# One projection unit for latent queries, keys and forget gates, and a router's weight sums by two wide products

## The chip, the cores and the metric

The kernel runs on one core of one Trainium2 chip. The metric is the device time of one execution in microseconds. Engines are TensorE (PE; its weight loads are PEld), VectorE (DVE), ScalarE (ACT), GpSimd (POOL) and SyncE (SP), which issues most DMAs.

## What is computed

A decoder trunk of two layers over 512 tokens of width 1024, in float32. Of each layer the parts that matter here are the input projection, from which the latents and forget gates come, and the router:

```python
def _mixing(x, w_in, b_forget, g_cq, g_ckv, w_uq, w_ukv, g_head, w_out):
    proj = x @ w_in                                   # 1024 x 4260
    p_sb, p_fox, p_mla, p_dil = jnp.split(proj, ...)
    q, k, v, f = jnp.split(p_fox, [hd, 2 * hd, 3 * hd], axis=-1)
    log_f = jax.nn.log_sigmoid((f + b_forget))        # 4 columns: forget gates
    c_q, c_kv, k_r = jnp.split(p_mla, [256, 384], axis=-1)   # 256, 128 and 32 columns
    q = (_rmsnorm(c_q, g_cq) @ w_uq)
    kv = (_rmsnorm(c_kv, g_ckv) @ w_ukv)
...
def _hier_moe(x, w_group, b_group, w_expert, b_expert, w1, w3, w2):
    g_logits = xf @ w_group + b_group                 # 4 groups
    e_logits = xf @ w_expert + b_expert               # 16 experts, top-1 group, top-2 inside
```

Four kinds of attention (stick-breaking, forgetting, latent, dilated) share the projection; then a norm, the routed experts, and a second norm.

## The kernel before

Tokens lie in four tiles of 128 (`NT`). The residual stream is held transposed, as xT, in two halves (a rounded part and the rest), and every weight piece is loaded by SP, split by `hi` (ScalarE) and `lo` (VectorE, a subtraction of two SBUF tiles) in `Stream.conv_to` (lines 547 to 567), and multiplied in three passes (`mm3`, line 394). A projection unit (`Unit`, line 727) is a block of columns of `w_in`; `unit_parts` (line 591) cuts it into pieces of 4 x 128 rows where it has up to 256 columns, else of 2 x 128. A unit of kind "tok" makes 24 products per token tile (8 row blocks, three passes), with xT as the weight of TensorE and the columns streamed.

`ORDER` (line 597) gives the units' order. Its first two are "cq" (256 columns: latent queries) and "ckv" (160: latent keys and the rotary key, with the 4 forget-gate columns copied behind them by ScalarE, 164 in all). `projections` (line 867) goes through `lists_` (lines 862 and 863): the first `N_MIX` units tile by tile (cq 0, ckv 0, cq 1, ...), then the other units one after the other. `un.begin()` asks for the conversion of all the unit's pieces and of one piece ahead; a unit's first tile therefore stands behind all of these in ScalarE's and VectorE's queues, though a product waits only for its own piece. `ev_latent` (line 804) copies a tile's bank to SBUF and sums its squares on ScalarE. Then `mla_rest` (line 1072) transposes the forget gates and goes on to the rotary keys, and `mla_prep` (line 1122) normalises both latents; both wait for the events of all four tiles. `fox_consts` waits for the unit that `FC_AT` names.

All order is made by a planner in the kernel (`Plan`, line 88) while the program is built. Each chain of work is a generator that yields what it needs (pages of SBUF, banks of PSUM, events); the planner keeps a clock for each engine by costs of its own and always runs the chain that could start first. Its choice fixes the order of every engine's queue. The projections are "fill": of chains that could start by now on TensorE, another one goes first. `convert_first` (line 1555) converts the first pieces of a layer as early as they come, four in layer 0, two in layer 1 (`FIRST_CONV`).

At the start of layer 1 the second norm of layer 0 (`second_norm`, line 1591) delivers xT tile by tile: eight transposes on TensorE, scale and shift and the two halves on ScalarE and VectorE (`second_norm_T`), while GpSimd makes the stored copy by a product and a sum over 1024 columns (`second_norm_out`), which may begin when the tile's transposes are done.

`router_weights` (line 1438) scales the router's 20 columns by the norm's gain and shift (`wg`, `wb`, 8 row blocks of 20 columns each) and sums them over all 1024 rows: a matrix of ones times each block, 16 products of 20 columns accumulated into one bank. The sums, `wsum`, are first read by the first norm (line 1513). A float32 product is two instructions on PE.

Nearly every row names line 250, where a helper records every instruction, so rows are told apart by tiles and shapes.

Of the kernel before, what the change touches and what calls it, by code (L numbers as in the profile page):

```python
# [14 lines left out]
OP = mybir.AluOpType  # L15
# [15 lines left out]
N_PAGES = 42  # L31
FC_AT = "ckv"
N_PG = 12
N_MIX = 2
MAX_ITEMS = 4
# [41 lines left out]
def trunk(ctx, tc, x, w_in, b_forget, g_cq, g_ckv, w_uq, w_ukv, g_head, w_out, ln1_g, ln1_b,  # L77
# [513 lines left out]
    def unit_parts(w, c0, n, extra=None):  # L591

        kn = 2 if n > 256 else 4
        return [ws.add(cols(w, c0, n, kn * i, kn), kn, n,
                       None if extra is None else extra[:, kn * i:kn * i + kn, :]) for i in range(8 // kn)]

    ORDER = ["cq", "ckv", "d1q", "d1k", "d1v", "sbq", "sbk", "sbv", "d23q", "d23k", "d23v", "fxq", "fxk", "fxv"]
    COL = {"sbq": (0, 256), "sbk": (256, 256), "sbv": (512, 256), "fxq": (768, 256), "fxk": (1024, 256),
           "fxv": (1280, 256), "cq": (C_CQ, 256), "ckv": (C_CKV, 160)}
    for j, s in enumerate("qkv"):  # L600
        COL[f"d1{s}"] = C_DIL + 768 * j, 256
        COL[f"d23{s}"] = C_DIL + 768 * j + 256, 512
    for l in range(L):
        for u in ORDER:
            win_u[l, u] = unit_parts(w_in[l], *COL[u], wfs[l] if u == "ckv" else None)
        wo = w_out[l].rearrange("(g k p) c -> g p k c", g=4, k=2)
# [100 lines left out]
    def attention(l, x_ready, xT, x_stored):  # L707
# [96 lines left out]
        def ev_latent(un, b, i):  # L804
            n, c = (256, 0) if un.u == "cq" else (128, 1)
            nc.scalar.activation(un.out[0][:, i, 0:b.shape[1]], b, AF.Copy)
            nc.scalar.activation(b[:, 0:n], b[:, 0:n], AF.Square, scale=float(n) ** -0.5,
                                 accum_out=lat_ss[:, 2 * i + c:2 * i + c + 1])

        kinds = {"cq": ("tok", 1, ev_latent), "ckv": ("tok", 1, ev_latent)}  # L810
        for u, n in (("d1", 1), ("d23", 2)):
# [55 lines left out]
        def projections():  # L867
            for u, i in lists_:
                un = U[u]
                evs = [x_ready[i]] if un.kind == "tok" and not un.perm else list(x_ready)  # L870
                yield Need(pages=un.pages, banks=1, evs=evs)
                un.begin()
                if un.kind == "tok":
                    b = bank([128, 164 if u == "ckv" else COL[u][1]])
                    un.mm(b, i, range(8))
                else:
                    b = bank([128, 512])
                    un.mm(b, i, range(4))
                    yield Need()
                    un.mm(b, i, range(4, 8))  # L880
                un.end(b, i)
# [190 lines left out]
        def mla_rest():  # L1072
            yield Need(pgs=2, banks=1, evs=[ev["ckv"]])
            ckt = U["ckv"].out[0]

# [46 lines left out]
        def mla_prep():  # L1122
# [3 lines left out]
            nc.gpsimd.dma_start(wqr, w_uq[l].rearrange("(k p) c -> p k c", p=128))  # L1126
            cqt, ckt = U["cq"], U["ckv"]
            yield Need(evs=[ev["cq"], ev["ckv"]])
            cqt, ckt = cqt.out[0], ckt.out[0]
            v, y = st(8), st(8)  # L1130
# [307 lines left out]
        def router_weights():  # L1438
# [6 lines left out]
            yield Need(banks=1)  # L1445
            b = bank([128, 2, 20])
            for n, w in enumerate((wg, wb)):
                for k in range(8):
                    nc.tensor.matmul(b[:, n], lhsT=full, rhs=w[:, k], start=n == 0 and k == 0, stop=n == 1 and k == 7)
            yield Need()  # L1450
            nc.vector.tensor_copy(wsum, b)
            nc.vector.tensor_tensor(wsum[:, 1], wsum[:, 1], br, op=OP.add)
# [239 lines left out]
    for l in range(L + 1):  # L1692
# [473 lines left out]
        def last_rows(last):  # L2166
# [13 lines left out]
            if l + 1 == L:  # L2180
                load_gb(last, nc.sync)
            else:
                ws.limit = win_u[l + 1, ORDER[2]][-1] + 1

# [233 lines left out]
```

## Time and profile before

| | |
|---|---|
| median of 3 runs | 1615.7 us (1611.23 to 1615.98) |
| the profiled execution's own time | 1619.65 us |
| its span, first to last instruction | 1617.7 us |
| PE busy | 1436.7 us, 89%, 7620 products |
| PE weight loads busy | 1164.3 us, 72% |
| DVE, ACT, POOL busy | 68%, 55%, 23% |
| mean granted clock of TensorE | 0.929 |

Attention of layer 0 runs up to about 330 us, its output projection, norm and routing to about 450, the experts to about 765; layer 1 follows in the same way. A granted clock of 1.00 is 2.4 GHz and 0.50 is 1.2 GHz. Busy shares are means over stages with different limits, so the rows below are read by stage. In a row of the timeline, merged instructions have one row; its start and the start of the next row are used for rates.

### The profile page before, as it was taken

How to read it: one execution, taken by the hardware profiler on the slowest of the kernel's cores; microseconds unless marked ns; L12 is line 12 of the kernel's file. 1: busy time of each engine (PE TensorE's matmuls, PEld its weight loads, DVE VectorE, ACT ScalarE, POOL GpSimd, SP SyncE). 2: the span in 40 equal slices, each digit the busy share in tenths (PEclk: the TensorE clock that was granted, in tenths of full speed). 3: DMA queues.
4: the chain of work that ended last, by engine and by line, in shares of the span. 5: the costliest groups of instructions: out<-in, count | busy, mean ns of one | idle time of the engine just before them, and what ended most of it. 6: DMA issues, size and time to landing. Idle time of an engine off the chain costs nothing. (4 is left out here: it accounts for less than half of the span.)

```text
span 1617.7 us, 22596 instructions
## 1 busy us (share of the span) xinstructions
PE 1436.7 (89%) x7620; PEld 1164.3 (72%) x7620; DVE 1099.8 (68%) x1967; ACT 890.5 (55%) x1695; POOL 368.7 (23%) x388
## 2 busy tenths in 40 slices
PE   7999989989799999888799998989786999899674
PEld 7988878878666767655699987878666667666453
DVE  4745575476686889977774546654658779898667
ACT  5435454434346888775543534545424477887553
POOL 2511120240412224311421112002204213323002
PEclk9989999999899999988798999989887999999797
DMA  9201211263579999985330102204545799999813
GB/s 266 65 1 41 89 42 40 83 232 143 195 264 319 370 379 356 377 318 173 105 90 23 40 27 92 65 21 134 213 166 195 263 355 382 386 347 385 302 34 130
DMA packets 120700, 303.54 MB, mean 188 GB/s; under 512 B 21982, under 2 KB 45230, under 8 KB 120568
## 3 DMA queue, kind: packets, MB, share of 16 engines
q1 hardware_dynamic: 106936, 269.74, 45.9%
q0 software_dynamic: 12448, 32.11, 7.1%
q8 instruction: 64, 1.05, 0.3%
q14 instruction: 68, 0.56, 0.1%
q10 hardware_dynamic: 1184, 0.08, 0.1%
HBM read 284.14 MB, written 27.33 MB: 193 GB/s over the span
## 5 line engine op out<-in xcount | busy, mean ns | idle before, releaser
L250 PE MATMUL bank<-page,page 128*128 128x512 f32 (+5 forms) x4480 | 983.1, 371 | 62.1 <-DVE page L250 35.0
L250 PEld LDWEIGHTS bank<-page,page 128*128 128x128 f32 (+2 forms) x4480 | 760.6, 203 | 197.9 <-DVE page L250 55.2
L250 DVE TENSOR_TENSOR page<-page,page 128x1024 fp32r<-128x1024 f32 (+3 forms) x470 | 525.7, 1163 | 154.3 <-ACT page L250 140.8
L250 ACT ACTIVATE page<-page 128x1024 fp32r<-128x1024 f32 (+3 forms) x454 | 436.2, 1021 | 49.1 <-DMA page<-in_w_in_dram 11.8
L250 PE MATMUL bank<-page,pg 128*128 128x64 f32 (+1 forms) x1360 | 317.0, 375 | 32.3 <-ACT page L250 14.7
L250 PEld LDWEIGHTS bank<-page,pg 128*128 128x128 f32 x1360 | 227.0, 202 | 115.1 <-issue 37.8
L250 ACT ACTIVATE page<-bank 64x512 fp32r<-64x512 f32 (+8 forms) x255 | 122.1, 506 | 197.1 <-PE bank L250 135.7
L250 ACT ACTIVATE pg<-bank 128x256 f32<-128x256 f32 (+6 forms) x223 | 101.4, 469 | 223.5 <-PE bank L250 221.6
L250 POOL DMA_INDIRECT yd<-page,xidx x30 | 67.5, 2249 | 403.3 <-ACT page L250 165.9
L250 DVE TENSOR_TENSOR page<-bank,page 128x512 fp32r<-128x512 f32 (+4 forms) x142 | 79.9, 599 | 65.9 <-ACT page L250 65.7
L250 POOL TENSOR_TENSOR page<-pg,pg 128x256 f32<-128x256 f32 (+1 forms) x56 | 51.1, 928 | 270.0 <-DVE pg L250 211.5
L250 PE MATMUL bank<-cid,pg 128*128 128x128 f32 (+2 forms) x500 | 84.2, 286 | 29.4 <-ACT pg L250 19.4
L250 POOL TENSOR_TENSOR page<-page,page 128x1024 f32<-128x1024 f32 (+4 forms) x32 | 63.1, 1971 | 153.4 <-ACT page L250 104.7
L250 PE MATMUL bank<-cid,page 128*128 128x128 f32 (+1 forms) x608 | 86.5, 280 | 10.5 <-DVE page L250 5.4
L250 PEld LDWEIGHTS bank<-cid,pg 128*128 128x128 f32 (+2 forms) x500 | 58.7, 147 | 46.2 <-ACT pg L250 25.1
L250 PEld LDWEIGHTS bank<-cid,page 128*128 128x128 f32 (+1 forms) x608 | 71.6, 143 | 24.9 <-DVE page L250 7.7
L250 ACT ACTIVATE pg<-pg 128x256 f32<-128x256 f32 (+5 forms) x146 | 68.6, 477 | 22.3 <-DVE pg L250 18.4
L250 POOL DMA_INDIRECT page<-x1d,xidx x30 | 54.5, 1818 | 42.4 <-DVE e_slots L250 17.9
L250 POOL CAST page<-page 64x512 fp32r<-64x512 f32 x48 | 29.9, 623 | 136.3 <-ACT page L250 102.8
L250 DVE COPY pg<-bank 128x256 f32<-128x256 f32 (+3 forms) x73 | 35.2, 484 | 28.4 <-PE bank L250 28.2
L250 DVE TENSOR_TENSOR pg<-bank,pg 64x512 f32<-64x512 f32 (+6 forms) x81 | 44.8, 559 | 11.9 <-ACT pg L250 10.8
L250 POOL MEMSET page<- 128x1024 f32 (+1 forms) x34 | 44.7, 1319 | 1.8 <-DVE page L250 1.8
(217 smaller groups left out, 974.4 us busy)
## 6 DMA issues: line engine op xcount, KB each, us to landing
page<-in_w_dram SPq DMA_DIRECT2D x396, 512.0 KB, 10.9
page<-in_w_in_dram SPq DMA_DIRECT2D x64, 512.0 KB, 4.1
page<-in_w_out_dram SPq DMA_DIRECT2D x16, 512.0 KB, 4.1
x1d<-page SPq DMA_DIRECT2D x8, 512.0 KB, 2.8
yd<-page SPq DMA_DIRECT2D x8, 512.0 KB, 5.1
page<-yd SPq DMA_DIRECT2D x8, 512.0 KB, 7.0
scr<-pg POOLq DMA_DIRECT2D x16, 132.0 KB, 2.0
pg<-scr POOLq DMA_DIRECT2D x16, 132.0 KB, 4.5
```

Of the source, the lines that this page charges most:

```text
L250: r = f(*args, **kw)
```

## The change

The units "cq" and "ckv" become one unit "lat" of 416 columns (they are neighbours in `w_in`) and the 4 forget-gate columns, 420 in all, in four pieces of 2 x 128 rows instead of two and two of 4 x 128. Its two output pages are those of the old units. `N_MIX` is 1, so `lists_` goes lat 0, lat 1, lat 2, lat 3. All that waited for one or both of the old events waits for the new one. The router's sums are made by two products of 160 columns (all eight blocks side by side), and VectorE adds the eight blocks from PSUM, where it copied 40 sums before.

```diff
--- before.py
+++ after.py
@@ -29,9 +29,9 @@
 RMS_EPS = 1e-6
 ALPHA = (2.0 * L) ** 0.25
 N_PAGES = 42
-FC_AT = "ckv"
+FC_AT = "lat"
 N_PG = 12
-N_MIX = 2
+N_MIX = 1
 MAX_ITEMS = 4
 AHEAD = 5
 SPARE = 1
@@ -594,15 +594,15 @@
         return [ws.add(cols(w, c0, n, kn * i, kn), kn, n,
                        None if extra is None else extra[:, kn * i:kn * i + kn, :]) for i in range(8 // kn)]
 
-    ORDER = ["cq", "ckv", "d1q", "d1k", "d1v", "sbq", "sbk", "sbv", "d23q", "d23k", "d23v", "fxq", "fxk", "fxv"]
+    ORDER = ["lat", "d1q", "d1k", "d1v", "sbq", "sbk", "sbv", "d23q", "d23k", "d23v", "fxq", "fxk", "fxv"]
     COL = {"sbq": (0, 256), "sbk": (256, 256), "sbv": (512, 256), "fxq": (768, 256), "fxk": (1024, 256),
-           "fxv": (1280, 256), "cq": (C_CQ, 256), "ckv": (C_CKV, 160)}
+           "fxv": (1280, 256), "lat": (C_CQ, 416)}
     for j, s in enumerate("qkv"):
         COL[f"d1{s}"] = C_DIL + 768 * j, 256
         COL[f"d23{s}"] = C_DIL + 768 * j + 256, 512
     for l in range(L):
         for u in ORDER:
-            win_u[l, u] = unit_parts(w_in[l], *COL[u], wfs[l] if u == "ckv" else None)
+            win_u[l, u] = unit_parts(w_in[l], *COL[u], wfs[l] if u == "lat" else None)
         wo = w_out[l].rearrange("(g k p) c -> g p k c", g=4, k=2)
         wout_u[l] = {(n, g): ws.add(wo[g, :, :, 512 * n:512 * n + 512], 2, 512)
                      for n, g in [(0, 0), (0, 2), (0, 3), (1, 0), (1, 2), (1, 3), (0, 1), (1, 1)]}
@@ -802,12 +802,13 @@
             split_k(un.out, i, b)
 
         def ev_latent(un, b, i):
-            n, c = (256, 0) if un.u == "cq" else (128, 1)
-            nc.scalar.activation(un.out[0][:, i, 0:b.shape[1]], b, AF.Copy)
-            nc.scalar.activation(b[:, 0:n], b[:, 0:n], AF.Square, scale=float(n) ** -0.5,
-                                 accum_out=lat_ss[:, 2 * i + c:2 * i + c + 1])
-
-        kinds = {"cq": ("tok", 1, ev_latent), "ckv": ("tok", 1, ev_latent)}
+            for o, c, w in zip(un.out, (0, 256), (256, 164)):
+                nc.scalar.activation(o[:, i, 0:w], b[:, c:c + w], AF.Copy)
+            for c, n in ((0, 256), (1, 128)):
+                nc.scalar.activation(b[:, 256 * c:256 * c + n], b[:, 256 * c:256 * c + n], AF.Square,
+                                     scale=float(n) ** -0.5, accum_out=lat_ss[:, 2 * i + c:2 * i + c + 1])
+
+        kinds = {"lat": ("tok", 2, ev_latent)}
         for u, n in (("d1", 1), ("d23", 2)):
             kinds[u + "q"] = kinds[u + "k"] = ("tok", n, ev_rope)
             kinds[u + "v"] = ("tok", n, ev_copy)
@@ -871,7 +872,7 @@
                 yield Need(pages=un.pages, banks=1, evs=evs)
                 un.begin()
                 if un.kind == "tok":
-                    b = bank([128, 164 if u == "ckv" else COL[u][1]])
+                    b = bank([128, 420 if u == "lat" else COL[u][1]])
                     un.mm(b, i, range(8))
                 else:
                     b = bank([128, 512])
@@ -1070,8 +1071,8 @@
         mla = {}
 
         def mla_rest():
-            yield Need(pgs=2, banks=1, evs=[ev["ckv"]])
-            ckt = U["ckv"].out[0]
+            yield Need(pgs=2, banks=1, evs=[ev["lat"]])
+            ckt = U["lat"].out[1]
 
             fb = bank([128, 512])
             for t in range(NT):
@@ -1124,9 +1125,8 @@
             wkr, wqr = page([128, 512]), page([128, 2, 384])
             nc.gpsimd.dma_start(wkr, w_ukv[l])
             nc.gpsimd.dma_start(wqr, w_uq[l].rearrange("(k p) c -> p k c", p=128))
-            cqt, ckt = U["cq"], U["ckv"]
-            yield Need(evs=[ev["cq"], ev["ckv"]])
-            cqt, ckt = cqt.out[0], ckt.out[0]
+            yield Need(evs=[ev["lat"]])
+            cqt, ckt = U["lat"].out
             v, y = st(8), st(8)
             rs_v(v, lat_ss, 1.0, RMS_EPS)
             rs_act(y, v)
@@ -1443,12 +1443,11 @@
             for o, s in ((wg, lng[l][0]), (wb, lnb[l][0])):
                 nc.vector.tensor_tensor(o, wr, s.unsqueeze(2).to_broadcast([128, 8, 20]), op=OP.mult)
             yield Need(banks=1)
-            b = bank([128, 2, 20])
+            b = bank([128, 2, 8, 20])
             for n, w in enumerate((wg, wb)):
-                for k in range(8):
-                    nc.tensor.matmul(b[:, n], lhsT=full, rhs=w[:, k], start=n == 0 and k == 0, stop=n == 1 and k == 7)
+                nc.tensor.matmul(b[:, n], lhsT=full, rhs=w, start=n == 0, stop=n == 1)
             yield Need()
-            nc.vector.tensor_copy(wsum, b)
+            nc.vector.tensor_reduce(wsum, b.rearrange("p n k c -> p n c k"), axis=AX.X, op=OP.add)
             nc.vector.tensor_tensor(wsum[:, 1], wsum[:, 1], br, op=OP.add)
             rel(b, full, wb)
 
@@ -2180,7 +2179,7 @@
             if l + 1 == L:
                 load_gb(last, nc.sync)
             else:
-                ws.limit = win_u[l + 1, ORDER[2]][-1] + 1
+                ws.limit = win_u[l + 1, ORDER[N_MIX]][-1] + 1
 
         def load_gb(last, q):
             last.gb = [page([128, D]) for _ in range(2)]
```

## Rows read from the trace of the kernel before

**Rows 1.** TensorE's waits, 0 to 400 us: waiter, released by, sum, times, longest.

```profile
PE bank L250 <- ACT pg L250: 12.9, 12, 5.6
PE bank L250 <- DVE page L250: 7.1, 5, 2.7
...
PE bank L250 <- ACT page L250: 3.2, 2, 2.6
PE bank L250 <- DVE pg L250: 1.0, 1, 1.0
```

**Rows 2.** TensorE's timeline, layer 0: start, length, operation, count, [idle before, released by].

```profile
10.71 4.32 PE L250 MATMUL bank<-page,page 128*128 128x256 f32 x23 [0.68 <-DVE page L250]
...
22.97 16.90 PE L250 MATMUL bank<-page,page 128*128 128x164 f32 x144
39.70 0.60 PE L250 MATMUL bank<-cid,page 128*4 128x128 f32 x4
40.06 3.11 PE L250 MATMUL bank<-page,page 128*128 128x256 f32 x24
43.01 0.60 PE L250 MATMUL bank<-cid,page 128*128 128x128 f32 x4
```

**Rows 3.** Busy time by stretch in the expert stage: PE, PEld, DVE, ACT, POOL, PEclk, DMA, GB/s.

```profile
600.00:700.00 100.00, 93.56 (x406) 66.14 (x405) 88.44 (x108) 80.84 (x106) 36.38 (x18) 1.00 0.99 368
```

**Rows 4.** TensorE's timeline at the start of layer 1.

```profile
767.50 1.88 PE L250 MATMUL bank<-page,cid 128*128 128x512 f32 x4
...
777.07 4.92 PE L250 MATMUL bank<-page,page 128*128 128x256 f32 x22 [3.21 <-DVE page L250]
781.82 1.04 PE L250 MATMUL bank<-cid,page 128*128 128x128 f32 x8
...
813.60 10.94 PE L250 MATMUL bank<-page,page 128*128 128x256 f32 x70 [3.23 <-DVE page L250]
824.38 0.60 PE L250 MATMUL bank<-cid,page 128*4 128x128 f32 x4
```

**Rows 5.** TensorE's timeline, twelve products of 512 columns and the row behind.

```profile
126.66 3.01 PE L250 MATMUL bank<-page,page 128*128 128x512 f32 x12
129.51 0.60 PE L250 MATMUL bank<-cid,page 128*96 128x128 f32 x4
```

**Rows 6.** TensorE's timeline at the router's weight sums, layer 0, then layer 1.

```profile
81.68 1.93 PE L250 MATMUL bank<-wg,pg 128*128 128x20 f32 x16
83.46 2.68 PE L250 MATMUL bank<-pg,pg 128*128 128x20 f32 x19
85.94 4.23 PE L250 MATMUL bank<-page,page 128*128 128x512 f32 x12
90.00 0.52 PE L250 MATMUL bank<-pg,pg 128*128 128x256 f32 x3
...
871.42 1.91 PE L250 MATMUL bank<-wg,pg 128*128 128x20 f32 x16
...
876.00 0.45 PE L250 MATMUL bank<-cid,pg 128*128 128x128 f32 x1
...
880.55 4.64 PE L250 MATMUL bank<-page,page 128*128 128x512 f32 x12
...
885.03 0.60 PE L250 MATMUL bank<-cid,pg 128*128 128x128 f32 x4
```

**Rows 7.** Busy time and granted clock (PEclk) of four short stretches.

```profile
866.00:868.00 2.00, 2.00 (x19) 1.84 (x18) 2.00 (x7) 0.73 (x4) 0.00 (x0) 1.00 0.00 0
87.00:88.00 1.00, 1.00 (x3) 0.78 (x3) 0.00 (x0) 0.00 (x0) 0.00 (x0) 0.50 0.00 0
877.00:878.00 1.00, 1.00 (x7) 0.91 (x6) 0.42 (x1) 0.66 (x2) 0.00 (x0) 0.50 0.00 0
816.00:818.00 2.00, 2.00 (x11) 2.00 (x11) 0.00 (x0) 0.00 (x0) 0.00 (x0) 0.50 0.63 177
```

**Rows 8.** VectorE's timeline, then GpSimd's, start of layer 1.

```profile
779.08 0.84 DVE L250 TENSOR_TENSOR page<-page,page 128x656 fp32r<-128x656 f32 x1
...
783.71 5.67 DVE L250 TENSOR_TENSOR page<-page,page 128x656 fp32r<-128x656 f32 x2 [0.52 <-ACT page L250]
...
783.00 5.30 POOL L250 TENSOR_TENSOR page<-page,page 128x1024 f32<-128x1024 f32 x2 [5.67 <-ACT page L250]
```

**Rows 9.** TensorE's timeline at the routing sums, layer 0, then layer 1.

```profile
444.79 0.19 PE L250 MATMUL bank<-asb,tri 128*128 128x16 bf16 x1 [9.77 <-DVE asb L250]
...
1239.54 0.19 PE L250 MATMUL bank<-asb,tri 128*128 128x16 bf16 x1 [10.03 <-DVE asb L250]
```

## What the change should do to the time

> **What bounds the kernel now.** I read the page's busy shares and its PE waits first, then TensorE's order of time around the two edits, then the clock of the same stretches, then the queues of VectorE and GpSimd at the start of layer 1.
>
> In the first 400 us TensorE waits some 24 us on other engines: 12.9 for ScalarE's softmax tiles, 7.1, 3.2 and 1.0 for others [rows 1]. From 22.97 to 39.70 and beyond, its rows follow one another with no wait shown [rows 2]. So in attention of layer 0 TensorE's own queue sets the pace, and work taken out of it should move what follows. The expert stage that comes after is busy on PE (93.56 of 100 us) and has its DMA full (share 0.99) [rows 3]; both are paced by buffers that earlier work gives back, so a shift made before it should pass through it, and I count it neither as a gain nor as a loss.
>
> The start of layer 1 is another matter. There TensorE waits again and again for VectorE (3.21 us before 777.07, 3.23 before 813.60) [rows 4]: the second norm delivers xT tile by tile, and the latent products of one tile are done before the next arrives. What is saved there is mostly saved on idle time.
>
> **Latent units.** Per token tile, 24 products of 256 columns and 24 of 164 become 24 of 420. In layer 0, 144 products, half of each width, take 16.73 us from 22.97 to 39.70: 232 ns a pair [rows 2]. 24 of 256 columns take 2.95 us from 40.06 to 43.01: 123 ns [rows 2]; so 164 columns cost 110, hardly less, which is why a merge pays at all. No row has 420 columns. Twelve of 512 take 2.85 us from 126.66 to 129.51: 237 ns [rows 5], an upper end; 512 columns scaled down in proportion give 195, the lower end; the line from 123 at 256 to 237 at 512 gives 196, which I take, as it lies on the two nearest widths. Saving 36 ns a pair (-5 to 37), 0.87 us a tile. For tiles 1 to 3 of layer 0 that is 2.6 us (-0.4 to 2.7). Tile 0 is paced by the weights' conversions: 23 products of 256 take 10.71 to about 14.9 after a wait for VectorE [rows 2], 181 ns each. Its four loads stay at the head of SP's queue and carry the same bytes (4 of 426 KB against 2 of 524 and 2 of 328). The wide unit needs all four pieces in its first tile where the narrow one needed two; the pieces keep their bytes (4 of 128x840 against 2 of 1024 and 2 of 656 words a partition), so their last one is converted at the same time. I take 0.4 us gain (-1 to 2). Layer 0: 3.0 us.
>
> ScalarE's and VectorE's conversions handle as many elements as before; two more copies of a few forget-gate columns a layer and the four evacuation operations now in one chain hang on banks that TensorE doesn't need next: nothing on the path, while TensorE has other banks; without that cover, under 1 us a layer. The waits on one event instead of two end where they did, since tile 3 of both units came last anyway.
>
> **Router weight sums.** 16 products of 20 columns (32 instructions on PE) become two of 160 (4). In layer 0 the old ones run from 81.68 to 85.94 with three products of 256 columns among them: 4.26 - 3 x 0.123 = 3.9 us; in layer 1 from 871.42 to 876.00, 4.6 us [rows 6]. TensorE does nothing else meanwhile, so this is path. The new price isn't in the trace: two float32 products of 512 columns take 1.88 us [rows 4], the upper end; two at the price of the narrow ones (3.9/16) 0.5, the lower; in proportion to the columns between these, 0.9. Gain 3.0 and 3.7 us.
>
> Behind the narrow products the clock falls. The granted clock is 1.00 at 866 to 868 and 0.50 at 877 to 878; in layer 0 it is 0.50 at 87 to 88 [rows 7]: half, the lower of its two levels, though PE was busy without a gap, with weight loads and 20 columns apiece. Twelve products of 512 columns then take 85.94 to 90.00, 4.06 us, and 880.55 to 885.03, 4.48 us [rows 6], against 2.85 [rows 5]: 1.2 and 1.6 lost. What runs from 876.00 to 880.55 is slowed too; at the ratio 4.48/2.85 its 4.55 us would be 2.9: 1.7 more. I expect the clock to stay up when the long run of narrow products is gone, since nothing else in these rows is thin: 1.2 + 3.3 us, with zero as the lower end if it falls anyway, and 1.2 + 3.9 as the upper (4.55 halved). Router in all: 4.2 us in layer 0, 7.0 in layer 1.
>
> The copy of 40 sums becomes a strided sum over 320 PSUM elements on VectorE; its result is read only at the first norm, hundreds of us later, so some 0.3 us more of VectorE is covered. Uncovered it would cost just that.
>
> **What passes through.** 3.0 + 4.2 + 7.0 = 14.2 us leave TensorE's queue in attention. Some will come back as waits for softmax tiles, which TensorE now meets earlier [rows 1]; half is my lower end, all the upper, three quarters my value, nearer to all because only 24 us in 400 are waits: 10.7 us (7.1 to 14.2).
>
> **Start of layer 1.** Here PE runs at half clock (0.50 at 816 to 818 [rows 7]): 22 products of 256 columns take 777.07 to 781.82, 216 ns each [rows 4]. At that level width is paid in full (216 scaled to 420 columns: 354, to 164: 138, together 354), so the merge saves nothing until the clock rises. Of the last tile and what follows it, 813.60 to 824.38 [rows 4], I count 0.6 us (0 to 0.9). The hand-over between tiles I put at zero: the transposes of tile 1 come at 781.82, behind the narrow query unit of tile 0, and would come behind the whole wide unit, 24 x (354 - 216) = 3.3 us later at that clock. Against this, the conversions of the second half, which now stand on VectorE between the transposes of tile 1 and the next xT (two subtractions in 5.67 us at 783.71, where one alone took 0.84 [rows 8]), are asked for at the start of the wide unit, ahead of GpSimd's 5.30 us of affine [rows 8], and run in idle time. The two are about equal. Ends: 9.9 us lost (3.3 three times), 6 us gained (5.67 less the 2.2 that two such subtractions take alone, at the first tile, and somewhat less at the other two together).
>
> Those two subtractions, of 656 and 1024 columns, took 5.67 us while GpSimd's two products took 5.30; one of 656 alone took 0.84, and scaled by width the pair would take 2.2 [rows 8]. The Trainium skill, SBUF — State Buffer, "Who interferes with whom", has it that a VectorE operation with two inputs in SBUF and a GpSimd operation that reads SBUF exclude each other for a whole instruction. The trace agrees (5.67 us against 2.2). By that rule two more subtractions of the wide unit would lose up to one affine operation each, 2 x 2.65 us, if they fell there; that is the wide-unit rival below with 5.3 us on top.
>
> **Sum.** 10.7 + 0.6 = 11.3 us off the profiled execution's 1619.65: 1608.4. That execution lies 4 us above the median of 1615.7, which gives 1604.4 as the median after.
>
> **Rivals.**
> - More comes through: the longer first unit lets the transposes of tiles 1 and 2 run together, the hand-over gains its 6 us and all 14.2 pass: 1615.7 - 14.2 - 0.6 - 6 = 1594.9. For it: the subtractions at 783.71 get out of GpSimd's way; against: no row shows the new order.
> - The edit of the router doesn't hold the clock up: 4.5 us less times three quarters, 1607.8. Against: the row at 866 to 868.
> - The gain goes back into softmax waits: a quarter passes, 3.6 + 0.6: 1611.5. For it: 12.9 us of such waits; against: they are few and far apart.
> - The wide unit stands before the transposes at half clock on three tiles: 9.9 us lost, 1614.3. For it: the rows at 777.07 and 781.82; against: the conversions that get out of the way.
> - Slower, by order. The planner sorts all queues by its own clock, which these edits move by several us a layer. What order is worth, the two layers show: from the transposes of the forget gates to the routing sums, the same work takes 405.1 us in layer 0 (39.70 to 444.79) and 415.2 in layer 1 (824.38 to 1239.54) [rows 2, 4, 9]: 10.1 us. The place is the interleaving of softmax items and projections in attention. One layer falling from the better to a worse order eats 10.1: 1614.5. If both do, 20.2 less 11.3: 1624.6. It decides from 16 us on, 11.3 and the 4.8 that can be told from nothing. Against it: a new order can as well be better, above all in layer 1.
>
> **How the numbers follow.** Forecast 0.46; more 0.12; clock falls anyway 0.07; back into waits 0.08; wide unit 0.08; worse order in one layer 0.08; in both 0.11. Under 0.3% (4.8 us) a measurement of this kernel can't be told from no change. The first three are faster: 0.65. The next three are within: 0.24. The last is slower: 0.11. The range goes from 1594 (just past the first rival) to 1618 (the wide unit's 1614.3 with the lower end of what passes, 3.6 us worse); the worse order in both layers and little else are left out.
>
> **What would show it.** Right: 96 latent products a layer near 196 ns in layer 0; four thin router instructions under 1.5 us and a granted clock of 1.00 after them in both layers; the forget gates' transposes 3 us earlier in layer 0; the routing sums some 6 us earlier after them in layer 0. Wrong: more TensorE wait for ScalarE's tiles by as much as was saved; a first tile of layer 1 whose next transposes come later than 5 us after its first product and xT that follows later; a longer way from 824 to the routing sums.

## The result

The changed kernel takes 1627.7 us as the median of six executions (1622.2 to 1632.6); the kernel before, beside it on the same chip, 1614.7 (1611.2 to 1618.7). The ratio is 1.008, with a 95% interval of 1.005 to 1.010: slower by 0.8%, where 1604.4 us had been forecast. The profiled execution of after took 1622.2, below its median, that of before 1619.65, above its own, so the two traces differ by less than the kernels do. In a second set of executions on another chip (below) the ratio was 1.012 [1.008, 1.015]. Three executions that lie far off, one of lat_good (4698.8 us), one of pin_pages (4703.2) and one of the kernel before beside them (1941.4), are left out of all medians.

TensorE has less to do, and finishes later. Its waits in the first 420 us, to be held against [rows 1], which read the same up to 420:

```profile
PE bank L250 <- ACT pg L250: 13.0, 10, 3.9
PE bank L250 <- ACT page L250: 9.2, 4, 3.6
PE bank L250 <- POOL page L250: 7.0, 7, 3.4
...
PE bank L250 <- DVE page L250: 3.8, 6, 1.7
PE bank L250 <- DVE pg L250: 2.9, 7, 0.7
```

ScalarE's softmax tiles (pg) cost what they did; 7.0 us of waits for GpSimd are new, and ScalarE's pages cost 6 us more. TensorE's timeline in layer 0, to be held against [rows 2, 6, 9]:

```profile
20.36 16.89 PE L250 MATMUL bank<-page,page 128*128 128x420 f32 x96
37.09 0.52 PE L250 MATMUL bank<-cid,page 128*4 128x128 f32 x3
38.71 0.27 PE L250 MATMUL bank<-cid,page 128*4 128x128 f32 x1 [1.11 <-ACT page L250]
...
86.18 0.44 PE L250 MATMUL bank<-wg,pg 128*128 128x160 f32 x2
86.45 0.43 PE L250 MATMUL bank<-pg,pg 128*128 128x160 f32 x2
86.62 3.02 PE L250 MATMUL bank<-page,page 128*128 128x512 f32 x12
89.48 0.60 PE L250 MATMUL bank<-cid,page 128*128 128x128 f32 x4
...
461.35 0.20 PE L250 MATMUL bank<-asb,tri 128*128 128x16 bf16 x1 [10.02 <-DVE asb L250]
```

The edits do their own work. The forget gates' transposes begin at 37.09 instead of 39.70, 2.6 us earlier. The four router instructions take 0.44 us (86.18 to 86.62), and the twelve products of 512 columns behind them 2.86 (to 89.48) instead of 4.06, at the upper clock (columns as in [rows 3]):

```profile
87.00:88.00 1.00, 1.00 (x6) 0.83 (x5) 0.92 (x1) 0.63 (x2) 0.00 (x0) 1.00 0.87 328
```

Yet the routing sums of layer 0 come at 461.35, 16.6 us later than in [rows 9]. What has changed is the order. The tile den_m holds the latent attention's softmax, m_str the mask of stick-breaking. These are their rows in layer 0: operation, tile, count, shortest/median/longest ns, first to last start. First those of the kernel before:

```profile
L250 DVE TENSOR_REDUCE den_m<-bank x16: 291/486/692, 133.3 to 168.6; 128x1 f32<-128x128 f32 x4, 128x1 f32<-128x256 f32 x4, 128x1 f32<-128x384 f32 x4, 128x1 f32<-128x512 f32 x4
L250 PE MATMUL bank<-m_str,cidb x16: 229/230/233, 175.8 to 250.3; 128*128 128x128 bf16 x16
```

And those of the changed kernel:

```profile
L250 DVE TENSOR_REDUCE den_m<-bank x16: 280/488/692, 232.2 to 282.8; 128x1 f32<-128x128 f32 x4, 128x1 f32<-128x256 f32 x4, 128x1 f32<-128x384 f32 x4, 128x1 f32<-128x512 f32 x4
L250 PE MATMUL bank<-m_str,cidb x16: 229/230/330, 157.2 to 229.4; 128*128 128x128 bf16 x16
```

Before, the latent attention goes first and stick-breaking follows; after, the latent attention starts 99 us later, behind stick-breaking. Six stretches of the changed kernel show what that does:

```profile
90.00:100.00 10.00, 4.51 (x24) 3.27 (x22) 6.79 (x14) 6.24 (x12) 5.00 (x8) 0.74 0.00 0
100.00:110.00 10.00, 9.07 (x47) 7.52 (x48) 3.26 (x10) 4.40 (x20) 0.00 (x0) 0.58 0.00 0
110.00:120.00 10.00, 8.38 (x71) 7.11 (x71) 4.41 (x12) 5.23 (x19) 0.00 (x0) 1.00 0.01 2
...
220.00:230.00 10.00, 4.96 (x23) 3.90 (x23) 9.62 (x16) 6.61 (x15) 0.00 (x0) 0.73 0.18 55
230.00:240.00 10.00, 9.24 (x44) 8.55 (x43) 5.78 (x15) 4.34 (x12) 0.00 (x0) 0.50 0.19 52
240.00:250.00 10.00, 8.25 (x33) 6.95 (x33) 4.03 (x7) 6.60 (x14) 0.00 (x0) 0.50 0.05 4
```

From 91.5 us on the sixteen neighbour items (the d1 branch) run with no projection between them, and TensorE waits for GpSimd's casts (5.5 us of the 7.0 above). It is busy for 4.51 of 10 us, and the granted clock falls towards its lower level (0.50, 1.2 GHz). The same comes again at 220 us, and from 230 to 250 us the latent items, begun late, run at 0.50.

Layer 1 keeps the order of its branches and gains. Its start and its routing sums, to be held against [rows 4, 9]:

```profile
792.47 6.96 PE L250 MATMUL bank<-page,page 128*128 128x420 f32 x22 [2.98 <-DVE page L250]
799.27 1.91 PE L250 MATMUL bank<-cid,page 128*128 128x128 f32 x16
...
825.78 6.20 PE L250 MATMUL bank<-page,page 128*128 128x420 f32 x40 [1.11 <-DVE page L250]
831.82 0.60 PE L250 MATMUL bank<-cid,page 128*4 128x128 f32 x4
...
1242.16 0.19 PE L250 MATMUL bank<-asb,tri 128*128 128x16 bf16 x1 [10.01 <-DVE asb L250]
```

From the row of 22 latent products of the first tile to the forget gates' transposes it takes 39.35 us (792.47 to 831.82), where before took 47.31 (777.07 to 824.38): 8.0 us. From there to the routing sums it takes 410.3 us instead of 415.2: 4.9. So layer 1 gains 12.9 us, and layer 0 loses 16.6 up to its routing sums.

### The profile page after: what moved, and what is told of

It is laid out like the page before. It is cut to its first block, busy times and chain, and to the rows that moved or that the text cites. A ratio compares the mean times of both kernels' runs of the same rounds, so it can differ in the third digit from the quotient of the medians.

```text
span 1620.5 us, 22123 instructions
## 1 busy us (share of the span) xinstructions
PE 1427.7 (88%) x7372; PEld 1148.8 (71%) x7372; DVE 1102.8 (68%) x1967; ACT 894.3 (55%) x1699; POOL 362.6 (22%) x388
## 5 line engine op out<-in xcount | busy, mean ns | idle before, releaser
L250 PE MATMUL bank<-page,page 128*128 128x512 f32 (+5 forms) x4288 | 969.1, 376 | 69.4 <-DVE page L250 30.2
L250 PEld LDWEIGHTS bank<-page,page 128*128 128x128 f32 (+1 forms) x4288 | 745.8, 201 | 210.2 <-DVE page L250 51.7
L250 DVE TENSOR_TENSOR page<-page,page 128x1024 fp32r<-128x1024 f32 (+4 forms) x470 | 526.0, 1165 | 144.2 <-ACT page L250 141.6
L250 ACT ACTIVATE page<-page 128x1024 fp32r<-128x1024 f32 (+3 forms) x454 | 435.7, 1021 | 52.5 <-DMA page<-in_w_in_dram 13.9
L250 PE MATMUL bank<-page,pg 128*128 128x64 f32 (+1 forms) x1360 | 321.8, 380 | 35.1 <-ACT page L250 14.1
L250 ACT ACTIVATE page<-bank 128x256 f32<-128x256 f32 (+8 forms) x255 | 120.8, 507 | 181.8 <-PE bank L250 120.8
L250 DVE TENSOR_TENSOR pg<-bank,pg 64x512 f32<-64x512 f32 (+6 forms) x81 | 44.9, 560 | 12.6 <-ACT pg L250 11.5
```

The source lines that it names most:

```text
L250: r = f(*args, **kw)
```

## The experiments

Two things could have cost layer 0 its time: the new operations themselves, or the order that the planner makes of all the work once these operations have other sizes and prices. The first experiments part the edits; the later ones change the order without the edits, and the edits without the order. Ratios are to the kernel before, run beside each.

**lat_only.** The router's sums go back to the old form:

```
-            b = bank([128, 2, 8, 20])
+            b = bank([128, 2, 20])
             for n, w in enumerate((wg, wb)):
-                nc.tensor.matmul(b[:, n], lhsT=full, rhs=w, start=n == 0, stop=n == 1)
+                for k in range(8):
+                    nc.tensor.matmul(b[:, n], lhsT=full, rhs=w[:, k], start=n == 0 and k == 0, stop=n == 1 and k == 7)
...
+            nc.vector.tensor_copy(wsum, b)
```

> The changed kernel with the router's sums as before (sixteen products of 20 columns and a copy); only the unit of 420 columns is kept. Theory 'order': the shorter latent stage alone turns layer 0 round (sixteen neighbour items alone from about 90 us, stick-breaking before the latent attention), so the loss stays and the router's gain is missing: 1628 to 1636 us, with the first score of the latent softmax near 232 us as in the changed kernel (133 us in the kernel before). Rival 'router': the loss comes from the two wide products or the sum over blocks; without them the latent unit's forecast gain is left: 1606 to 1612 us.

Measured: 1633.7 us, ratio 1.012 [1.010, 1.015]; the first latent score is at 241.4. The loss is there without the router's edit, so it comes with the wide unit. (Its layer 1 comes in yet another order: from the forget gates' transposes to the routing sums it takes 405.4 us, with the old sums, 846.16 to 1251.53.)

**router_only.** The kernel before with the new router sums (the reverse of the diff above).

> The kernel before with the two products of 160 columns and the sum over blocks; latents in two units as before. Theory 'order': layer 0 keeps its order (latent attention before stick-breaking) and the router's 3.0 and 3.7 us and the clock behind it (1.2 and 3.3 us) come out at least in part: 1606 to 1612 us, granted clock 1.00 behind the router in both layers. Rival 'narrow': the clock falls behind the router as before and the few us are swallowed: 1614 to 1616 us. Rival 'router' (the loss is the router's): about 1625 us.

Measured: 1592.4 us, ratio 0.986 [0.983, 0.988]: 24 us faster, more than any theory had. Layer 0 ends 22.3 us earlier (routing sums at 422.50), and the latent attention starts at 118.7 instead of 133.3. The removed 4 us can't be all of that, so the order was suspected here too, this time in the kernel's favour.

**router_old_price.** The same kernel, but the planner still charges the old price for the sums, and so gives every engine the order of the kernel before:

```
+                if dt == F32 and n == 160:
+                    return 8 * (0.85 * m + 2.0)
                 if dt == F32:
...
+            plan.clock["DVE"] -= 292.0
             nc.vector.tensor_reduce(wsum, b.rearrange("p n k c -> p n c k"), axis=AX.X, op=OP.add)
```

> The kernel before with the new router sums, while the planner goes on charging them at the old price (eight products of 20 columns for each wide one, and the old copy), so that every engine gets its instructions in exactly the order of the kernel before. What is left is the direct effect of the router edit. Theory 'order' (most of the 24 us that the new sums alone brought in layer 0 came with another order of the work): 1602 to 1610 us, with layer 1 some 8 us shorter as with the new sums alone and layer 0 shorter by 4 to 7 us only. Rival 'direct' (the gain is the edit's own, passed on through the waits): 1590 to 1596 us. Rival 'swallowed': 1614 us or more.

Measured: 1604.7 us, ratio 0.992 [0.989, 0.995], 11.5 us faster. Its timeline at the router in layer 0 and at the two routing sums:

```profile
82.70 0.51 PE L250 MATMUL bank<-wg,pg 128*128 128x160 f32 x2
83.04 0.79 PE L250 MATMUL bank<-pg,pg 128*128 128x160 f32 x5
83.67 2.90 PE L250 MATMUL bank<-page,page 128*128 128x512 f32 x12
86.41 0.52 PE L250 MATMUL bank<-pg,pg 128*128 128x256 f32 x3
...
440.22 0.19 PE L250 MATMUL bank<-asb,tri 128*128 128x16 bf16 x1 [9.53 <-DVE asb L250]
...
1227.58 0.20 PE L250 MATMUL bank<-asb,tri 128*128 128x16 bf16 x1 [10.01 <-DVE asb L250]
```

From the first sum to the end of the twelve wide products it is 3.71 us (82.70 to 86.41), against 8.32 in [rows 6]: 4.6 us, and the routing sums come 4.6 us earlier (440.22 against 444.79). In layer 1, from the forget gates' transposes (819.50 in this trace) to the routing sums, it is 408.1 us against 415.2: 7.1. So the edit itself is worth 11.7 us, nearly what was measured, and the 12 us between this kernel and the last are order. One place where that order gains can be seen, from 100 to 110 us; first the kernel before, then router_only:

```profile
100.00:110.00 10.00, 6.80 (x38) 5.50 (x38) 4.33 (x14) 4.20 (x14) 0.91 (x2) 0.79 0.01 2
```

```profile
100.00:110.00 10.00, 9.90 (x86) 9.12 (x85) 5.41 (x17) 5.99 (x21) 0.92 (x2) 1.00 0.01 2
```

So the kernel before has a thin stretch of its own among the neighbour items, and router_only has not.

**sbfirst_b.** None of the change's edits; in layer 0 of the kernel before the latent items wait for stick-breaking's:

```
-            yield Need(evs=[ev["krope"]])
+            yield Need(evs=[ev["krope"]] + ([on("sbgo")] if l == 0 else []))
...
             oall[0] = page([128, NT, 256])
+            on("sbgo").set()
```

> The kernel before with none of the change's edits; in layer 0 alone the latent attention's items are held until stick-breaking's items are there, so stick-breaking goes first while the neighbour items still run among the projections. Theory 'stick-breaking first costs the time': 1626 to 1634 us, with the granted clock low between 215 and 260 us as in the changed kernel. Rival 'the neighbour items alone cost it': 1614 to 1620 us. Rival 'order is worth nothing by itself': 1614 to 1618 us.

Measured: 1640.7 us, ratio 1.015 [1.012, 1.018]: 24.5 us slower with the same arithmetic, more than any theory had. Its latent scores, the routing sums of layer 0, and TensorE's waits from 200 to 300 us:

```profile
L250 DVE TENSOR_REDUCE den_m<-bank x16: 281/486/692, 230.3 to 280.5; 128x1 f32<-128x128 f32 x4, 128x1 f32<-128x256 f32 x4, 128x1 f32<-128x384 f32 x4, 128x1 f32<-128x512 f32 x4
```

```profile
PE bank L250 <- ACT pg L250: 5.0, 2, 3.9
PE bank L250 <- ACT page L250: 1.3, 1, 1.3
PE bank L250 <- DVE pg L250: 1.0, 2, 0.7
PE bank L250 <- DVE page L250: 0.4, 1, 0.4
```

```profile
230.00:240.00 10.00, 9.24 (x45) 8.56 (x44) 5.70 (x15) 2.56 (x10) 0.00 (x0) 0.50 0.08 27
240.00:250.00 10.00, 8.25 (x30) 6.70 (x30) 5.63 (x8) 8.07 (x17) 0.00 (x0) 0.54 0.19 52
```

That is the changed kernel's layer 0 almost row for row: latent scores from 230.3 (232.2), the half clock from 230 to 250, and in the changed kernel the same four waits from 200 to 300 (5.4, 1.3, 1.0, 0.4). The routing sums come at 460.25, there at 461.35. Stick-breaking first, by itself, is enough to make a layer as late as that: 15.5 us behind [rows 9] in these two profiled executions.

**hold_b.** None of the change's edits; in layer 0 the transposes of the neighbour keys wait for the stick-breaking queries, so that the neighbour items come alone:

```
-            yield Need(pages=n, banks=1, evs=[ev[part_of(u)[0]]])
+            evs = [ev[part_of(u)[0]]]
+            if l == 0 and u == "d1k":
+                evs.append(ev["sbq"])
+            yield Need(pages=n, banks=1, evs=evs)
```

> The kernel before with none of the change's edits; in layer 0 alone the transposes of the neighbour keys wait until the stick-breaking queries are projected, so the sixteen neighbour items come in one run without projections between them, while the latent attention still goes ahead of stick-breaking. Theory 'neighbour items alone cost time': 1622 to 1630 us. Rival 'stick-breaking first is what costs': 1614 to 1620 us.

Measured: 1619.6 us, ratio 1.002 [0.999, 1.006], executions from 1610.8 to 1627.5. It can't be told from the kernel before, and its executions are spread over 16.6 us. The latent scores still start at 133.0. But the run says little on the hole at 90 us: its own thin stretch (7.10 of 10 us busy from 100 to 110) is about that of the kernel before (6.80), not that of the changed kernel (4.51). It shows only that neighbour items alone need not cost more than neighbour items among projections.

**pin_sbk.** The changed kernel, with stick-breaking's items in layer 0 held until the latent attention's are there:

```
+            ev["mla"].set()
             last = countdown(16, lambda: rel(*mq[0], *mq[1], *mk[0], *mk[1], mv))
...
-            yield Need(pages=1, evs=[ev["sbq"], ev["sbk"], ev["sbv"]])
+            yield Need(pages=1, evs=[ev["sbq"], ev["sbk"], ev["sbv"], ev["mla"]])
```

(The wait holds in both layers; in layer 1 that is the order anyway.)

> The changed kernel; in layer 0 stick-breaking's items are held until the latent attention's are there, so the latent attention goes first again, while the sixteen neighbour items still come in one run without projections between them. Theory 'stick-breaking first costs the time': some 10 to 17 us of the changed kernel's time come back, 1610 to 1618 us. Rival 'the neighbour items alone cost it': 1624 to 1630 us, as the changed kernel.

Measured: 1649.1 us, ratio 1.019 [1.016, 1.022]. Both theories missed. Holding stick-breaking back brings the latent scores from 232.2 to 168.9 only, not to the 133.3 of the kernel before, and stick-breaking, which could have run meanwhile, starts at 223.6.

```profile
80.00:120.00 40.00, 33.26 (x159) 27.35 (x158) 18.64 (x39) 17.77 (x49) 5.00 (x8) 0.69 0.10 27
120.00:160.00 40.00, 39.73 (x219) 35.76 (x219) 11.73 (x29) 11.26 (x27) 7.56 (x12) 0.80 0.05 14
```

So "latent attention first" was too short a name for what is lost. The runs below fit with this: what counts is that its items are there early, while projections are left to lie between them.

**pin_sbq.** The changed kernel, with the projection of the stick-breaking queries in layer 0 held until the neighbour keys are transposed:

```
                 evs = [x_ready[i]] if un.kind == "tok" and not un.perm else list(x_ready)
+                if l == 0 and u == "sbq":
+                    evs.append(ev["d1kT"])
```

> The changed kernel, with one more condition in layer 0: the stick-breaking queries are projected only after the transposes of the neighbour keys, so the keys get their four pages first and the neighbour items run among the projections again, with the latent attention ahead of stick-breaking. All arithmetic as in the changed kernel. Theory 'order': the 16.6 us that layer 0 lost come back, 1602 to 1612 us, latent softmax first near 140 us. Rival 'unit' (the latent unit or the sums are slow in themselves): 1622 us or more. Rival 'half' (the order recovers, but the stalls of the neighbour items have another cause): 1613 to 1620 us.

Measured: 1611.4 us, ratio 0.997 [0.996, 0.999], latent scores from 135.0. Beside the changed kernel's 1627.7 that is 16 us back, at the upper end of what "order" had expected.

**pin_pages.** As pin_sbq, but the queries wait only until the keys' transposes have been given their four pages:

```
+                if l == 0 and u == "sbq":
+                    evs.append(on("d1kp"))
...
             o = rT[u] = [page([128, 2, 512], dt) for _ in range(n)]
+            if u == "d1k":
+                on("d1kp").set()
```

> The changed kernel with every edit kept; in layer 0 the stick-breaking queries only wait until the transposes of the neighbour keys have their four pages, so the neighbour items run among the projections, but stick-breaking still goes ahead of the latent attention. Theory 'stick-breaking first is the price': as the changed kernel, 1622 to 1632 us. Rival 'neighbour items alone are the price': 1608 to 1616 us.

Measured: 1619.4 us, ratio 1.001 [0.999, 1.004], between the theories.

```profile
90.00:100.00 10.00, 10.00 (x67) 8.84 (x67) 6.69 (x19) 6.38 (x21) 0.00 (x0) 1.00 0.00 0
100.00:110.00 10.00, 10.00 (x68) 8.70 (x67) 3.92 (x9) 4.98 (x17) 2.44 (x4) 1.00 0.01 2
...
230.00:240.00 10.00, 9.25 (x44) 8.47 (x44) 5.09 (x13) 2.91 (x11) 0.00 (x0) 0.50 0.00 1
```

The hole at 90 us is gone (10.00 of 10 at full clock), so the neighbour items lie among the projections again; the half clock at 230 is still there, as stick-breaking still goes first (latent scores from 229.0).

**lat_good.** pin_pages, and the latent preparation in layer 0 taken ahead of equal rivals:

```
-        plan.spawn(mla_prep())
+        plan.spawn(mla_prep(), first=9 if l else 1)
```

> The changed kernel with every edit kept; in layer 0 the latent preparation is taken ahead of equal rivals, and the stick-breaking queries wait until the transposes of the neighbour keys have their four pages. The latent attention then stands ahead of stick-breaking, with its items among the projections. Theory 'order': with the order mended the edits' own gains show: 1582 to 1600 us, the first score of the latent softmax before 135 us. Rival 'unit in layer 0' (the unit of 420 columns costs time in layer 0 whatever the order, as the time with the queries pinned alone, 1611 us, would also allow): 1608 to 1620 us.

Measured: 1603.2 us, ratio 0.993 [0.990, 0.996], latent scores from 119.5. That is 3 us above what "order" had expected and 5 below its rival.

```profile
230.00:240.00 10.00, 10.00 (x63) 9.11 (x62) 6.32 (x15) 3.93 (x10) 0.00 (x0) 1.00 0.00 0
240.00:250.00 10.00, 10.00 (x48) 9.69 (x47) 4.51 (x6) 8.28 (x15) 0.00 (x0) 1.00 0.23 56
```

Every edit of the change is in this kernel. Against pin_pages one argument differs, and 16.2 us; against the changed kernel beside it (next), 32.

**after_again.** The changed kernel once more, as a base for these runs.

> The changed kernel as it is, on the chip of these runs, as their base and for a second profiled execution. Both theories: 1622 to 1633 us; layer 0 ends (first routing sum) near 461 us again, and what differs between its executions lies in an expert stage.

Measured: 1635.5 us (1633.8 to 1637.4), somewhat above what was expected. The expectation on the expert stage was wrong: in this profiled execution the routing sums of layer 0 come at 474.88, 13.5 us later than in the first profile of the same kernel, so the difference is in layer 0; 9.5 of them are there at the first stick-breaking mask (166.7 against 157.2).

```profile
100.00:110.00 10.00, 9.13 (x43) 7.53 (x42) 2.98 (x9) 3.84 (x16) 0.00 (x0) 0.50 0.00 0
110.00:120.00 10.00, 9.68 (x46) 8.50 (x45) 2.88 (x7) 2.97 (x11) 0.00 (x0) 0.50 0.01 2
120.00:130.00 10.00, 9.73 (x46) 8.25 (x45) 2.55 (x6) 4.08 (x13) 0.00 (x0) 0.50 0.00 0
...
474.88 0.19 PE L250 MATMUL bank<-asb,tri 128*128 128x16 bf16 x1 [10.41 <-DVE asb L250]
```

Behind the hole of 90 to 100 us the clock stays at its lower level through 130 us here; in the first profile it is back by 110. The instructions and their order are the same. So the hole at 90 us has a price that differs from execution to execution.

**lat_l1.** The wide unit in layer 1 only, two units in layer 0; the new router sums in both:

```
+LAT_IN = (1,)
...
-    ORDER = ["lat", "d1q", "d1k", "d1v", "sbq", "sbk", "sbv", "d23q", "d23k", "d23v", "fxq", "fxk", "fxv"]
+    REST = ["d1q", "d1k", "d1v", "sbq", "sbk", "sbv", "d23q", "d23k", "d23v", "fxq", "fxk", "fxv"]
...
+    ORDERS = [["lat"] + REST if l in LAT_IN else ["cq", "ckv"] + REST for l in range(L)]
```

> The changed kernel with the unit of 420 columns in layer 1 alone; layer 0 projects cq and ckv as two units as before; router sums new in both layers. Theory 'order': layer 0 keeps the order of the kernel before, layer 1 keeps the gain that the pair of traces showed (8 us at its start, some 5 behind it): 1596 to 1606 us. Rival 'latent unit': the unit of 420 columns is itself what costs time: 1615 us or more. Rival 'nothing in layer 1' (the gain seen there belongs to the two executions, not to the unit): as with the router alone, 1606 to 1612 us.

Measured: 1582.5 us, ratio 0.982 [0.977, 0.987]; faster than expected and than both kernels of this study. The median is 9.9 us below the router alone (1592.4), but these are four executions of each, and they overlap (1579.7 to 1595.3, and 1588.9 to 1600.3). What the wide unit gains at the start of layer 1 is clearer in the traces: from the row of 22 latent products (753.43) to the forget gates' transposes (792.25) it takes 38.8 us, as in the changed kernel, and 46.6 in router_only (765.93 to 812.57). The eight traces with the wide unit in layer 1 lie from 37.1 to 39.5 us, the five with two units from 46.6 to 47.6. It is the version to keep.

The placing of the work in layer 0 beside the time (us; first latent score, first stick-breaking mask and routing sums of layer 0 from the profiled execution):

| kernel | latent | stick-breaking | routing sums | median |
|---|---|---|---|---|
| lat_l1 | 119.1 | 160.7 | 421.94 | 1582.5 |
| router_only | 118.7 | 160.3 | 422.50 | 1592.4 |
| lat_good | 119.5 | 171.2 | 436.14 | 1603.2 |
| router_old_price | 129.6 | 172.2 | 440.22 | 1604.7 |
| pin_sbq | 135.0 | 175.4 | 449.71 | 1611.4 |
| pin_pages | 229.0 | 142.3 | 460.94 | 1619.4 |
| hold_b | 133.0 | 174.7 | 436.04 | 1619.6 |
| changed kernel | 232.2 | 157.2 | 461.35 | 1627.7 |
| lat_only | 241.4 | 165.9 | 469.70 | 1633.7 |
| after_again | 242.5 | 166.7 | 474.88 | 1635.5 |
| sbfirst_b | 230.3 | 155.4 | 460.25 | 1640.7 |
| pin_sbk | 168.9 | 223.6 | 486.94 | 1649.1 |

Where the latent scores start by 135 us, the routing sums come by 450; where they start later, at 460 or after. (The profiled execution of hold_b took 1613.2, 6 us under its median.)

## Why the prediction failed

**Router sums: right, and better than the pass-through allowed.** Forecast 4.2 us in layer 0 and 7.0 in layer 1; with the order held, 4.6 and 7.1 (in layer 1 of the changed kernel 4.9 are left of them). The clock stays up behind the two wide products, as expected: the twelve products take 2.86 us in the changed kernel. The two wide products were put at 0.9 us and take 0.44; the upper end for them, 1.88 us, is 1.32 when read from the starts of its row and the next (767.50 and 768.82).

**What passes through: too low.** Three quarters were taken; with the order held, 11.7 us left the two layers and 11.5 were measured. Next to nothing came back as waits for softmax tiles: with the order held TensorE waits 12.5 us for them up to 420 us, 12.9 in [rows 1].

**Latent units in layer 0: right by themselves.** The 96 products from 20.36 to 37.09 are 72 of 420 columns and 24 of 256; with 123 ns for these [rows 2], 420 columns take 191 ns (forecast 196). The transposes come 2.6 us earlier (forecast 3.0).

**Start of layer 1: wrong by 7 us.** Forecast 0.6, measured 8.0. The hand-over put at zero is a gain: the transposes of the next tiles now run together (sixteen at 799.27, eight at 781.82 in [rows 4]), and behind the last wait 40 products are left before the transposes (70 in [rows 4]), 6.0 us instead of 10.8. The other 3.2 us: the last wait ends 33.3 us after the row of 22 products (825.78), where it ended 36.5 after it (813.60). The conversions did get out of GpSimd's way, but the xT of later tiles now meets it; VectorE's rows in the changed kernel:

```profile
794.63 3.21 DVE L250 TENSOR_TENSOR page<-page,page 128x840 fp32r<-128x840 f32 x3 [0.29 <-ACT page L250]
...
804.56 8.70 DVE L250 TENSOR_TENSOR page<-page,page 128x256 fp32r<-128x256 f32 x7 [1.02 <-ACT page L250]
```

Three subtractions of 840 columns take 3.21 us while GpSimd computes nothing, where two took 5.67 in [rows 8]; seven of 256 then take 8.70 beside GpSimd's four products (10.39 us from 800.45). That the hand-over gains 6 us and that all of the rest passes was the rival "more comes through"; apart from the order of layer 0 it is what happened. The other rivals on the faster side or within 0.3% (the clock falls anyway, back into waits, the wide unit ahead of the transposes) did not come true.

**The order: the step that failed.** The sum held only if the order held: a change of order stood in it at nothing and was left to a rival. The rival "slower, by order" had the mechanism and the place, but its price of 10.1 us a layer was the difference between two layers of one kernel, and with that price it needed both layers. One wait added in layer 0 alone costs 24.5 us (sbfirst_b), 15.5 of them by its routing sums in the two profiled executions, and the same freedom is worth 12 us the other way (router_only beside router_old_price). Two layers in the same order (latent attention first in both) show nothing of what an order outside them costs. The chances should have been wide on both sides, with a price from rows where such an order would leave TensorE thin: the half clock and the waits of [rows 1] were there to be scaled.

The profiled executions add up: 16.6 us lost in layer 0, 1.2 gained in its experts (331.1 us from the routing sums to the row of 22 latent products, 332.3 before), 8.0 and 4.9 gained in layer 1; that leaves 2.5 of the 2.8 us between the two spans (1620.5 and 1617.7). In the profile of the second set layer 0 is 30.1 us late (474.88) and layer 1 gains 12.7; its span is 1634.5. So layer 0's loss differs from execution to execution, between 16.6 and 30.1 us in these two, and the medians (13.0 and 19.6 us slower) follow it.

What becomes of the 7.2 us that the edits free in layer 0 (2.6 and 4.6) is not shown. The hole at 90 us doesn't explain it: pin_pages has the edits and no such hole, and its routing sums (460.94) come no earlier than those of sbfirst_b (460.25), which has none of the edits. What the hole adds can only be bounded: beside pin_pages' 460.94 the changed kernel's two profiles are 0.4 and 13.9 us later, and its median beside it 16 us (1635.5).

**Why the order turned.** In the code, the neighbour keys' transposes ask for four pages, the latent queries' weights and results for four more, and the projection of the stick-breaking queries for its own; who comes first holds them. Letting the keys have their pages first mends the hole at 90 us (pin_pages), and the latent preparation's place in the queue brings the latent attention back ahead of stick-breaking (lat_good); these two are shown. That the latent preparation comes later with one unit in place of two can be seen in the trace as well: its first transposes come at 50.34 in the changed kernel, 43.01 in [rows 2]. They wait for VectorE's scaling of the latents, here in the kernel before, then in the changed kernel:

```profile
41.60 1.93 DVE L250 TENSOR_SCALAR page<-page,st 128x128 f32<-128x128 f32 x8
```

```profile
48.26 1.93 DVE L250 TENSOR_SCALAR page<-page,st 128x128 f32<-128x128 f32 x8
```

The evacuations in one chain on ScalarE are not the reason: their last sum of squares starts at 39.35 before and at 39.37 after. The delay arises in VectorE's queue: its next step on these sums starts at 41.00 before, as soon as ScalarE has given its input; after, that input is there at 42.34 and the step starts at 47.09, behind the forget gates, a conversion and other work. Why the planner put these ahead was not parted.

The wide unit in layer 0 was not measured in exactly the order of the kernel before; with lat_good (436.14 at the routing sums) still 13.6 us behind router_only, it stays open whether it can pay there.

## What to carry to other kernels

Where a planner sorts the queues by its own prices, an edit has two effects: its own, which can be read from the rows, and the new order, which can't and may be as large or larger, with either sign (here 12 us gained and 24.5 lost). Part them: run the edit with the planner still charging the old price, and run the old kernel in the other order. And before a forecast, see which requests stand a few us apart for the same buffers, since those are the ones that turn round.

## What the hardware showed

- The lower clock lasts differently long behind the same hole: with the same instructions the granted clock is back at 110 us in one profiled execution and stays at 0.50 through 130 in another. The routing sums of the layer differ by 13.5 us (461.35 and 474.88), of which 9.5 are there by the first stick-breaking mask (157.2 and 166.7).
- In the changed kernel the granted clock falls (0.73 from 220 to 230 us) while TensorE is busy for 4.96 of 10 us, and stays at 0.50 from 230 to 250, where it is busy for 9.24 and 8.25 of 10 us.
- Two products of 160 float32 columns, with the same sums as sixteen of 20, take 0.44 us instead of 3.9, and the granted clock behind them is 1.00 (87 to 88 us), where it was 0.50 behind the sixteen in [rows 7].
- VectorE's subtractions of two SBUF tiles stretch while GpSimd multiplies SBUF tiles: seven of 256 columns took 8.70 us at 804.56, where four took 1.42 at 792.00 while GpSimd issued only DMAs.
